# A two-layer encoder trunk in float32: gate projections by seven block products, up projections unit by unit, and memory products a step after their bank

## The chip, the cores and the metric

The kernel runs on one core of one Trainium2 chip. The metric is the device time in microseconds of one execution. Before the change the median of three runs is 2235.18 us (2234.59 to 2235.61).

## What is computed

Layer 0 is a mixer (a bidirectional mLSTM with 4 heads and a bidirectional RG-LRU) and a SwiGLU FFN, layer 1 is dilated sliding-window attention with 16 heads and a SwiGLU FFN. The change touches the FFN of both layers and the heads of the mLSTM. Cut to that:

```python
D_MODEL = 2048; SEQ = 256
D_FF = ((8 * D_MODEL + 3 * 256 - 1) // (3 * 256)) * 256      # 5632

def swiglu(h, w1, w3, w2):
    return (jax.nn.silu(h @ w1) * (h @ w3)) @ w2

def reference(x, ...):
    for l in range(DEPTH):                                   # DEPTH = 2
        ...                                                  # mixer or attention
        h = rmsnorm(x, f_norm[l])
        x = x + swiglu(h, f_w1[l], f_w3[l], f_w2[l])
    return rmsnorm(x, final_norm)

# in the mLSTM, for each head and direction
    s = jnp.einsum('bhld,bhsd->bhls', qj, kj) * w_intra
    num = jnp.einsum('bhls,bhsv->bhlv', s, vj) + ...
    h = num / jnp.maximum(jnp.abs(den), jnp.exp(-m_out))[..., None]
```

## The kernel before

All weights are float32. A weight block comes from memory as a unit `raw` of 512 rows by 512 columns (four row blocks of 128, 1 MB) and is split in two halves, each of two row blocks, into a high part `wh` (ACT casts it to fp32r, L205) and a low part `wl` (DVE subtracts, L206). Activations are held transposed and split in the same way, `xT`, with 256 tokens. A product is then three matmuls, high by high, high by low, low by high (`narrow`, L273 to L275): the stationary operand is a 128 by 128 block of the activations, the moving one 512 columns of the weights. One half of a unit is a **step**: two row blocks, two blocks of 128 tokens, three matmuls, twelve in all. Blocks whose output is wanted transposed go the other way round (L295, L296).

The program is written out step by step, and every engine runs its instructions in that order. `emit_step` (L277) first emits the splits up to three steps ahead (`AHEAD = 3`; `emit_split`, L192), then the step's matmuls, then it lets the open tasks run one piece each (`run_tasks`). The tasks are generators; a `yield` puts what follows behind the next step. What evacuates a chunk is such a task. The buffers of `wh` and `wl` are four each, so the split of step s + 4 waits for the matmuls of step s; those of `raw` are four too, and a load is issued on SP's queue when one is given back (`emit_load`).

An FFN (`ffn`, L920) has eleven chunks of 512 columns of w1 and w3. Chunk by chunk, all four units of w1 are taken, then all four of w3. `up1` (L924) evacuates w1: ACT applies Silu, scaled by the row norm `rstd`, into `up`. `up3` (L940) evacuates w3: DVE multiplies (L948), PE transposes (`hTp`), ACT and DVE split the result into `hT` (L961, L962). `UPS` cuts the eleven chunks into two passes, (0, 6) and (6, 11): after each, w2 is multiplied with the chunks made so far, for the four column groups of the output, and added to the residual `xres`. PSUM has eight banks: four for accumulators `acc` (two to a narrow chunk), two for transposes, two (`mx`) for small products, which a lock (`take`, `give`) hands from task to task.

In the mixer, `ml_head` (L673) makes for each head the products `qkp` and `nMb`, and later four products `num`. A task takes the lock, multiplies into the next of the two `mx` banks, reads the bank a step later and gives the lock back, then lets one step pass (`lag`).

Of the kernel before, what the change touches and what calls it, by code (L numbers as in the profile page):

```python
# [9 lines left out]
F32 = mybir.dt.float32  # L10
F32R = mybir.dt.float32r
AF = mybir.ActivationFunctionType
ALU = mybir.AluOpType
# [4 lines left out]
P = 128  # L18
KB = D // P
CW = 512  # L20
# [4 lines left out]
RB = 8  # L25
AH = 16
DH = 128
UPS = ((0, 6), (6, 11))
EPS = 1e-6
BIG = 1e30  # L30

# [3 lines left out]
C_N = 160  # L35


RAW_BUFS = 4
SPLIT_BUFS = 4
AHEAD = 3  # L40

SLOTS = 8
SLOT = 2112
EV_BUFS = 6
M4_BUFS = 6

CONC = 3
# [9 lines left out]
class Chunk:  # L57
    def __init__(self, evac):
        self.acc = None
        self.at_once = getattr(evac, "at_once", False)  # L60
        self.evac = evac

# [2 lines left out]
def trunk_kernel(ctx: ExitStack, tc: tile.TileContext, a, out):  # L65
# [37 lines left out]
    def mx(name="mx"):  # L103
        return mxp.tile([P, CW], F32, tag="mx", name=name)
# [3 lines left out]
    def lag():  # L108

        for _ in range(LAG):  # L110
            yield

    def take():

        while held["mx"]:
            yield
        held["mx"] = True
# [70 lines left out]
            pos["load"] += 1  # L188

    splits = {}  # L190

    def emit_split(s):  # L192

        st = steps[s]
        it = st["item"]
        raw = loaded[it][:, 2 * st["half"]:2 * st["half"] + 2, :]
        hi = whp.tile([P, 2, CW], F32R, tag="wh", name="wh")
        lo = wlp.tile([P, 2, CW], F32R, tag="wl", name="wl")
        for k in (0, 1) if s < 2 else (slice(0, 2),):
            if s < 2:  # L200
                use_xT(2 * s + k)
            elif s < KB // 2:
                use_xT(2 * s)
                use_xT(2 * s + 1)
            A.copy(hi[:, k], raw[:, k])  # L205
            V.tensor_tensor(lo[:, k], raw[:, k], hi[:, k].bitcast(F32), op=ALU.subtract)  # L206
        splits[s] = (hi, lo)
        if st["last_half"]:
            loaded.pop(it)
            emit_load()  # L210

    def add_unit(src, ch, kb0, first, last, act):

        items.append(wload(src, len(items)))
        it = len(items) - 1
        for h in range(2):
            steps.append({
                "item": it, "half": h, "last_half": h == 1, "ch": ch, "kb": kb0 + 2 * h, "act": act,
                "first": first and h == 0, "last": last and h == 1, "wide": False, "before": None,
            })  # L220

    def add_chunk(src, n_kg, act, evac, kgs=None):
        ch = Chunk(evac)
        for j, kg in enumerate(kgs or range(n_kg)):
            add_unit(src[kg], ch, 4 * kg, j == 0, j == n_kg - 1, act)
        return ch

    def add_blocks(units):

        for i in range(0, len(units), 2):  # L230
            pair = []
            for src, act, evac in units[i:i + 2]:
                items.append(wload(src, len(items)))
                pair.append((len(items) - 1, Chunk(evac), act))
            for h in range(2):
                for it, ch, act in pair:
                    steps.append({
                        "item": it, "half": h, "last_half": h == 1, "ch": ch, "kb": 8 * h, "act": act,
                        "first": h == 0, "last": h == 1, "wide": True, "before": None,
                    })  # L240

    urgent, queue, active = [], [], []
# [16 lines left out]
    def until(flag):  # L259
        n = 0  # L260
        while flag not in flags:
            run_tasks()
            n += 1
            assert n < 10000, flag

    def narrow(st, hi, lo, toks):
        for j in range(2):
            x2 = st["act"](st["kb"] + j)
            f, e = st["first"] and j == 0, st["last"] and j == 1
            for t in toks:  # L270
# [3 lines left out]
                PE.matmul(acc, xh, lo[:, j, :], start=False, stop=False)  # L274
                PE.matmul(acc, xl, hi[:, j, :], start=False, stop=e)  # L275

    def emit_step(s):  # L277
# [8 lines left out]
        hi, lo = splits.pop(s)  # L286
        if ch.acc is None:
            ch.acc = [accp.tile([P, CW], F32, tag="acc", name="acc") for _ in range(1 if st["wide"] else 2)]
        if st["wide"]:
            acc = ch.acc[0]  # L290
            wh, wl = (w.rearrange("p a (b f) -> p (a b) f", f=P) for w in (hi, lo))
            for j in range(8):
                x2 = st["act"](st["kb"] + j)
                f, e = st["first"] and j == 0, st["last"] and j == 7
                PE.matmul(acc, wh[:, j, :], x2.rearrange("p a b -> p (a b)"), start=f, stop=False)  # L295
                PE.matmul(acc[:, :S], wl[:, j, :], x2[:, 0, :], start=False, stop=e)  # L296
        else:
# [375 lines left out]
    def ml_head(h):  # L673
# [44 lines left out]
        for d in range(2):  # L718
            for t in range(2):
                yield from take()  # L720
                num = mx("num")[:, :DV + 1]
                pairs = [(3 * d + 2 * t, t)]
                if t != d:
                    pairs.append((3 * d + 1, d))
                for j, (blk, s) in enumerate(pairs):
                    PE.matmul(num, w6[:, blk, :], v[:, s, h, :DV + 1], start=j == 0, stop=j == len(pairs) - 1)  # L726
                yield
                r = sm(2, "den")
                V.tensor_scalar(
                    r[:, 0:1], num[:, DV:], -1.0, em[:, t, 4 * d + h:4 * d + h + 1], op0=ALU.mult, op1=ALU.max  # L730
                )
                V.tensor_tensor(r[:, 1:2], r[:, 0:1], num[:, DV:], op=ALU.max)
                V.reciprocal(r[:, 1:2], r[:, 1:2])
                hd = ml["h"][:, t, h, :]
                if d == 0:
                    A.mul(hd, num[:, :DV], r[:, 1:2])
                else:
                    V.scalar_tensor_tensor(hd, num[:, :DV], r[:, 1:2], hd, op0=ALU.mult, op1=ALU.add)
# [181 lines left out]
    def ffn(l, gains, nxt):  # L920
# [3 lines left out]
        def up1(c):  # L924
            def gen(ch):
                while f"rstd{gains}" not in flags:
                    yield
                es = []
                for t in range(2):
                    e = ev("up")  # L930
                    A.activation(e, ch.acc[t], AF.Silu, scale=cur["rstd"][:, t:t + 1])
                    es.append(e)
                ch.acc = None
                st["e", c] = es
                flags.add(f"up{l}_{c}")
                yield

            return gen
# [32 lines left out]
        def act_h(kb):  # L971
            until(f"h{l}_{kb}")
            return st["h", kb // 4][:, kb % 4]

        for hidx, (c0, c1) in enumerate(UPS):
# [3 lines left out]
            if hidx == 1:  # L979
                ssq = const.tile([P, 2, NCD], F32, name=f"ssq{l}")  # L980
            for n in range(NCD):
                if hidx == 0:
# [9 lines left out]
                add_chunk(a["w2"][l, n], c1 - c0, act_h, evac, kgs=range(c0, c1))  # L992
        return ssq


# [116 lines left out]
    n = NCD - 1  # L1112
    ch = steps[-1]["ch"]
    ends = [splits.pop(s) for s in range(len(steps) - tail, len(steps))]
    r = const.tile([P, 2], F32, name="rstd_f")
    for t in range(2):
        for st, (hi, lo) in zip(steps[-tail:], ends):
# [97 lines left out]
```

## Time and profile before

| | before |
|---|---|
| median of three runs | 2235.18 us |
| the profiled execution, its own time | 2238.2 us |
| its span | 2236.4 us |
| mean granted clock of TensorE | 0.996 |
| mixer up to the first FFN's first step | to about 375 us |
| FFN of layer 0, up to its last transposes | to about 1111 us |
| attention, up to the second FFN's first step | to about 1498 us |
| memory read over the span | 413.56 MB, 186 GB/s |

The stages are read from the transposes `nT`, which follow the last column group of each norm. PE is TensorE's matmul, PEld its weight load, DVE is VectorE, ACT ScalarE, POOL GpSimd, SP the engine that issues the loads. In a group of the profile stand the line, the engine, the operation, the tiles written and read, the shape and the count, then the busy time, the mean duration in ns, the idle time ahead of it and who ended that. In a timeline the first two numbers are start and duration in us. In a list of waits they are the total, the number and the longest in us. In a row of windows stand the window, its length, the busy time and number of instructions of each engine, the granted clock, the share of DMA and GB/s. In a row of loads stand the size of one load and the median time from issue to landing.

### The profile page before, as it was taken

The numbers are of one execution on the slowest core, as the hardware profiler recorded it, in microseconds if no ns is written. First come the engines' busy times: TensorE is split into PE (matmuls) and PEld (weight loads), VectorE is DVE, ScalarE is ACT, GpSimd is POOL, SyncE is SP. The second block draws the span as 40 slices with busy tenths as digits, with TensorE's granted clock in tenths as the row PEclk, the third lists the DMA queues.
The fourth block names the chain that finished last, engine by engine and source line by source line (L and its number), as shares of the span: only waits on it lengthen the run. The fifth ranks groups of instructions, "written<-read, shape, count | busy, mean of one in ns | idle before, by whom it ended". The sixth has DMA issues, their size and how long they took to land.

```text
span 2236.4 us, 25910 instructions
## 1 busy us (share of the span) xinstructions
PE 2217.9 (99%) x10412; PEld 1849.4 (83%) x10412; DVE 1246.7 (56%) x1516; ACT 1045.8 (47%) x1343; POOL 21.0 (1%) x37
## 2 busy tenths in 40 slices
PE   9999999999999999999999999999999999999998
PEld 7887888888888888888888888888888888888886
DVE  6876665445544444455566666564445444444554
ACT  6666545444443344444454555454444433444443
POOL 0000000000000000000000000000000000000000
PEclk9999999999999999999999999999999999999999
DMA  7443565555555555555555555555555556555553
GB/s 299 170 142 132 183 204 181 192 192 192 182 196 191 190 189 191 193 192 176 194 190 173 193 178 176 176 173 197 193 191 188 188 188 210 189 197 192 192 188 113
DMA packets 61457, 417.34 MB, mean 187 GB/s; under 512 B 7061, under 2 KB 7957, under 8 KB 12569
## 3 DMA queue, kind: packets, MB, share of 16 engines
q1 hardware_dynamic: 58616, 406.69, 53.4%
q0 software_dynamic: 2288, 8.39, 1.0%
q8 instruction: 81, 1.33, 0.2%
q10 hardware_dynamic: 432, 0.61, 0.1%
q14 instruction: 40, 0.32, 0.0%
HBM read 413.56 MB, written 2.10 MB: 186 GB/s over the span
## 4 chain that ended last, share of the span: by engine, by line
PE 94%; ACT 2%; DVE 2%; issue 1%; DMA 0%; SPq 0%; POOL 0%; POOLq 0%; DVEq 0%; ACTq 0%
PE acc L273 26%; PE acc L275 26%; PE acc L274 26%; PE acc L295 9%; PE acc L296 4%; ACT wh L205 1%; PE hTp L142 1%; DVE wl L206 1%; PE rgp L456 0%; PE nT L142 0%; PE apT L142 0%; DMA raw<-in_w_v 0%; PE num L726 0%; DVE xres L346 0%; PE asc L862 0%
## 5 line engine op out<-in xcount | busy, mean ns | idle before, releaser
L206 DVE TENSOR_TENSOR wl<-raw,wh 128x1024 fp32r<-128x1024 f32 (+1 forms) x770 | 940.4, 1222 | 851.6 <-ACT wh L205 849.2
L205 ACT CAST wh<-raw 128x1024 fp32r<-128x1024 f32 (+1 forms) x770 | 806.1, 1049 | 876.5 <-PE acc L275 795.0
L273 PE MATMUL acc<-wh,xT 128*128 128x512 f32 x1664 | 658.1, 396 | 0.9 <-ACT wh L205 0.9
L274 PE MATMUL acc<-wl,xT 128*128 128x512 f32 x1664 | 650.8, 391 | 1.2 <-DVE wl L206 1.2
L275 PE MATMUL acc<-wh,xT 128*128 128x512 f32 x1664 | 650.9, 391 | 0.0
L273 PEld LDWEIGHTS acc<-wh,xT 128*128 128x128 f32 x1664 | 313.8, 189 | 66.5 <-ACT wh L205 1.6
L274 PEld LDWEIGHTS acc<-wl,xT 128*128 128x128 f32 x1664 | 314.0, 189 | 65.9 <-DVE wl L206 2.6
L275 PEld LDWEIGHTS acc<-wh,xT 128*128 128x128 f32 x1664 | 313.6, 188 | 66.1
L295 PE MATMUL acc<-xT,wh 128*128 128x512 f32 x896 | 322.1, 402 | 0.5 <-ACT v L663 0.5
L273 PE MATMUL acc<-wh,hT 128*128 128x512 f32 x704 | 275.5, 391 | 0.0
L275 PE MATMUL acc<-wh,hT 128*128 128x512 f32 x704 | 274.4, 390 | 0.0
L274 PE MATMUL acc<-wl,hT 128*128 128x512 f32 x704 | 274.2, 389 | 0.0
L296 PE MATMUL acc<-xT,wl 128*128 128x256 f32 x896 | 251.7, 281 | 0.0
L295 PEld LDWEIGHTS acc<-xT,wh 128*128 128x128 f32 x896 | 168.5, 188 | 40.0 <-ACT v L663 0.6
L296 PEld LDWEIGHTS acc<-xT,wl 128*128 128x128 f32 x896 | 169.6, 189 | 0.9 <-DVE wl L206 0.3
L275 PEld LDWEIGHTS acc<-wh,hT 128*128 128x128 f32 x704 | 132.2, 188 | 27.5
L274 PEld LDWEIGHTS acc<-wl,hT 128*128 128x128 f32 x704 | 132.2, 188 | 27.2
L273 PEld LDWEIGHTS acc<-wh,hT 128*128 128x128 f32 x704 | 132.2, 188 | 27.0
L961 ACT CAST hT<-hTp 128x512 fp32r<-128x512 f32 x44 | 25.8, 587 | 83.2 <-PE hTp L142 83.2
L962 DVE TENSOR_TENSOR hT<-hTp,hT 128x512 fp32r<-128x512 f32 x44 | 30.4, 692 | 55.1 <-ACT hT L961 55.1
L273 PE MATMUL acc<-wh,oT 128*128 128x512 f32 x128 | 50.7, 396 | 0.0
L275 PE MATMUL acc<-wh,oT 128*128 128x512 f32 x128 | 50.0, 391 | 0.0
(222 smaller groups left out, 1206.4 us busy)
## 6 DMA issues: line engine op xcount, KB each, us to landing
raw<-in_w SPq DMA_DIRECT2D x264, 1024.0 KB, 4.8
raw<-in_w_aqk SPq DMA_DIRECT2D x32, 1024.0 KB, 4.8
raw<-in_w_out SPq DMA_DIRECT2D x16, 1024.0 KB, 4.9
raw<-in_w_av SPq DMA_DIRECT2D x16, 1024.0 KB, 4.8
raw<-in_w_o SPq DMA_DIRECT2D x16, 1024.0 KB, 4.8
raw<-in_w_xr SPq DMA_DIRECT2D x8, 1024.0 KB, 6.4
raw<-in_w_qk SPq DMA_DIRECT2D x8, 1024.0 KB, 4.8
raw<-in_w_og SPq DMA_DIRECT2D x8, 1024.0 KB, 4.9
```

What stands on the lines that cost most here:

```text
L142: PE.transpose(o, i, ident[:n, :n])
L205: A.copy(hi[:, k], raw[:, k])
L206: V.tensor_tensor(lo[:, k], raw[:, k], hi[:, k].bitcast(F32), op=ALU.subtract)
L273: PE.matmul(acc, xh, hi[:, j, :], start=f, stop=False)
L274: PE.matmul(acc, xh, lo[:, j, :], start=False, stop=False)
L275: PE.matmul(acc, xl, hi[:, j, :], start=False, stop=e)
L295: PE.matmul(acc, wh[:, j, :], x2.rearrange("p a b -> p (a b)"), start=f, stop=False)
L296: PE.matmul(acc[:, :S], wl[:, j, :], x2[:, 0, :], start=False, stop=e)
L961: A.copy(h[:, 2 * p:2 * p + 2, 0, :], ps)
L962: V.tensor_tensor(h[:, 2 * p:2 * p + 2, 1, :], ps, h[:, 2 * p:2 * p + 2, 0, :].bitcast(F32), op=ALU.subtract)
```

## The change

**Gate projections.** For the chunks 1 to 10 of w1 and the last three of its four units (`SEVEN`), a step is a 2 by 2 block product (two blocks of tokens, two row blocks, two halves of 256 columns) by Winograd's form of Strassen's scheme: seven block products in place of eight, each three matmuls of 256 columns. Four sums of weight blocks are made per unit (`weight_sums`; one stays in `raw`, three are split into `wf`), and four sums of activation blocks once per layer (`act_sums`, split into `sf`). Two further accumulators `ext` hold the shared products, and `up1` joins the four before Silu.

**Order of the up projections.** Units of w1 and w3 alternate; the accumulators of w3 lie in the two `mx` banks. `UPS` has four passes. In each, the last chunk's units of w2 come after the others' for the first two column groups.

**Buffers.** `raw` three for four, `ev` ten for six. The final gain is loaded 16 steps before the end and not 90.

**Memory products.** In `ml_head` the `lag` stands behind `take` and no longer behind `give`, and there is one more ahead of `qkp`.

```diff
-UPS = ((0, 6), (6, 11))
+UPS = ((0, 3), (3, 6), (6, 9), (9, 11))
+SEVEN = (1, 2, 3)
-RAW_BUFS = 4
+RAW_BUFS = 3
-EV_BUFS = 6
+EV_BUFS = 10
...
+    def weight_sums(it):
+        w = loaded[it]
+        b11, b12, b21, b22 = (w[:, i::2, 256 * j:256 * j + 256] for i in range(2) for j in range(2))
+        t1, t2, t4 = ts = [ev("ws").rearrange("p (a b) -> p a b", a=2) for _ in range(3)]
+        V.tensor_tensor(t1, b12, b11, op=ALU.subtract)
+        V.tensor_tensor(b12, b22, b12, op=ALU.subtract)
+        V.tensor_tensor(t2, b22, t1, op=ALU.subtract)
+        V.tensor_tensor(t4, b21, t2, op=ALU.subtract)
+        sums[it] = []
+        for t in ts:
+            f = m4((4, 256), "wf", F32R).rearrange("p (i a) b -> p i a b", i=2)
+            A.copy(f[:, 0], t)
+            V.tensor_tensor(f[:, 1], t, f[:, 0].bitcast(F32), op=ALU.subtract)
+            sums[it].append(f)
...
     def emit_split(s):
+        if st["seven"] and st["half"] == 0:
+            weight_sums(it)
...
+        todo = [
+            (a(a1, 0), b(0, 0), e0, 0), (sa(0), tb(0), e0, 1), (sa(1), tb(1), e1, 0), (sa(2), b(0, 1), e1, 1),
+            (a(a2, 0), b(1, 0), c0, 0), (sa(3), b(1, 1), c0, 1), (a(a2, 1), tb(2), c1, 0),
+        ]
+        for (xh, xl), (wh, wl), dst, n in ([todo[k] for k in (1, 0, 3, 2, 5, 4, 6)] if st["last"] else todo):
+            o = dst[:, n * 256:n * 256 + 256]
...
+            PE.matmul(o, xh, wh, start=new, stop=False)
+            PE.matmul(o, xh, wl, start=False, stop=False)
+            PE.matmul(o, xl, wh, start=False, stop=end)
...
         yield from take()
+        yield from lag()
         ps = mx("qkp")
...
                 yield from take()
+                yield from lag()
                 num = mx("num")[:, :DV + 1]
...
                 give()
-                yield from lag()
...
+                if ch.ext:
+                    A.copy(x0, e0)
+                    V.tensor_tensor(u2, e1[:, l_], x0[:, l_], op=ALU.add)
+                    V.tensor_tensor(x1[:, l_], e1[:, r_], u2, op=ALU.add)
+                    V.tensor_tensor(x1[:, r_], x1[:, l_], x0[:, r_], op=ALU.add)
+                    V.tensor_tensor(x0[:, r_], x0[:, r_], u2, op=ALU.add)
+                    V.tensor_tensor(x0, c0, x0, op=ALU.add)
+                    V.tensor_tensor(x1, c1, x1, op=ALU.add)
...
+        def act_sums():
+            for g in SEVEN:
...
+                for j, kb in enumerate((4 * g, 4 * g + 2)):
+                    V.tensor_tensor(vv, x[:, :, 0, :], x[:, :, 1, :], op=ALU.add)
+                    V.tensor_tensor(w[:, 0], a21, a22, op=ALU.add)
+                    V.tensor_tensor(w[:, 2], a11, a21, op=ALU.subtract)
+                    V.tensor_tensor(w[:, 1], w[:, 0], a11, op=ALU.subtract)
+                    V.tensor_tensor(w[:, 3], a12, w[:, 1], op=ALU.subtract)
+                    A.copy(f[:, :, 0, :], w)
+                    V.tensor_tensor(f[:, :, 1, :], w, f[:, :, 0, :].bitcast(F32), op=ALU.subtract)
+                    yield
...
-                add_chunk(a["w1"][l, c], 4, act, up1(c))
-                add_chunk(a["w3"][l, c], 4, act, up3(c))
+                for g in range(4):
+                    add_unit(a["w1"][l, c][g], chs[0], 4 * g, g == 0, g == 3, act,
+                             seven if c and g in SEVEN else None)
+                    add_unit(a["w3"][l, c][g], chs[1], 4 * g, g == 0, g == 3, act)
...
+            for n, kgs in ((0, range(c0, c1 - 1)), (1, range(c0, c1 - 1)), (0, (c1 - 1,)), (1, (c1 - 1,)),
+                           (2, range(c0, c1)), (3, range(c0, c1))):
...
+        steps[at_first]["before"] = lambda: queue.append(act_sums())
...
-    steps[-90]["before"] = load_fg
+    steps[-16]["before"] = load_fg
```

The emitted order shows the change at three places. The first is DVE at the start of the first FFN. The rows `xT` are the last norm's transposes being split, and each `wl` is the split of one step. Before:

```order
L346 TENSOR_TENSOR xres<-acc,xres 128x512 x2
L206 TENSOR_TENSOR wl<-raw,wh 128x1024
L373 SCALAR_TENSOR_TENSOR xT<-nT,cpk,xT 128x256 x4
L380 TENSOR_REDUCE rstd_3182<-ssq_o_115 128x2
L381 TENSOR_SCALAR rstd_3182<-rstd_3182 128x2
L206 TENSOR_TENSOR wl<-raw,wh 128x1024 x16
```

And now (`sa`, `sb` and `sf` belong to the sums of the activations):

```order
L441 SCALAR_TENSOR_TENSOR xT<-nT,cpk,xT 128x256 x4
L448 TENSOR_REDUCE rstd_3180<-ssq_o_115 128x2
L449 TENSOR_SCALAR rstd_3180<-rstd_3180 128x2
L1067 TENSOR_TENSOR sa<-xT 128x512
L1070 TENSOR_TENSOR sb<-sa 128x128
L1071 TENSOR_TENSOR sb<-sa 128x128
L1072 TENSOR_TENSOR sb<-sb,sa 128x128
L1073 TENSOR_TENSOR sb<-sa,sb 128x128
L1075 TENSOR_TENSOR sf<-sb,sf 128x4x128
L229 TENSOR_TENSOR wl<-raw,wh 128x1024
```

The rows from `sa` to `wl` follow six times; one set of sums now stands ahead of each of the splits of the FFN's steps 4 to 9, where sixteen splits followed each other before.

The second is DVE behind the end of a chunk (`up` is the gating, `hT` the split of the transposed result). Before:

```order
L206 TENSOR_TENSOR wl<-raw,wh 128x1024 x16
L948 SCALAR_TENSOR_TENSOR up<-acc,rstd_3182,up 128x512 x2
L206 TENSOR_TENSOR wl<-raw,wh 128x1024 x2
L962 TENSOR_TENSOR hT<-hTp,hT 128x2x256
L206 TENSOR_TENSOR wl<-raw,wh 128x1024
```

And now, from the joining of the accumulators on (`ws` and `wf` are the sums of weight blocks and their split):

```order
L1008 TENSOR_TENSOR up<-acc,up 128x512
L1009 TENSOR_TENSOR up<-acc,up 128x512
L229 TENSOR_TENSOR wl<-raw,wh 128x1024 x2
L1027 SCALAR_TENSOR_TENSOR up<-acc,rstd_3180,up 128x512 x2
L202 TENSOR_TENSOR ws<-raw 128x512
L203 TENSOR_TENSOR raw<-raw 128x2x256
L204 TENSOR_TENSOR ws<-raw,ws 128x512
L205 TENSOR_TENSOR ws<-raw,ws 128x512
L210 TENSOR_TENSOR wf<-ws,wf 128x512 x3
L229 TENSOR_TENSOR wl<-raw,wh 128x1024 x2
L1041 TENSOR_TENSOR hT<-hTp,hT 128x2x256
```

Six additions (the last two are shown) come ahead of two splits, and seven instructions between the gating and the next split.

The third is PE in the mixer, between the last `num` of one head and the `qkp` and `nMb` of another, where `nMb` goes into the bank that this `num` was in. Before, the rows that end the step between them:

```order
L273 MATMUL acc_1622<-wh_1550,xT_99 128x512
L274 MATMUL acc_1622<-wl_1551,xT_99 128x512
L275 MATMUL acc_1622<-wh_1550,xT_99 128x512
L682 MATMUL qkp_1664<-qkT_981 128x256 x2
L685 MATMUL nMb_1667<-nMs_798,ehr_97 128x512 x2
```

And now:

```order
L300 MATMUL acc_1604<-wh_1671,xT_99 128x512
L301 MATMUL acc_1604<-wl_1672,xT_99 128x512
L302 MATMUL acc_1604<-wh_1671,xT_99 128x512
L524 MATMUL rgp_1778<-xc_469,rgw_1442 128x256 x2
L751 MATMUL qkp_1784<-qkT_979 128x256 x2
L754 MATMUL nMb_1787<-nMs_796,ehr_97 128x512 x2
```

Before, `num_1640` stands twelve matmuls of `acc` ahead of `qkp_1664`. Now `num_1721` stands 24 ahead of `qkp_1784`, with two pairs of `rgp` (the RG-LRU's gates) between.

More of the change, by code (lines that the diff above doesn't have):

```diff
@@ L59, in __init__ @@
         self.acc = None
+        self.ext = None
+        self.small = False
         self.at_once = getattr(evac, "at_once", False)
@@ L207, in emit_split @@
         splits[s] = (hi, lo)
+        if st["seven"]:
+            splits[s] = (hi, lo, [t[:, :, st["half"]] for t in sums[it]])
+            if st["last_half"]:
+                sums.pop(it)
         if st["last_half"]:
@@ L210, in emit_split, with add_unit @@
             emit_load()
-    def add_unit(src, ch, kb0, first, last, act):
+    def add_unit(src, ch, kb0, first, last, act, seven=None):
         items.append(wload(src, len(items)))
@@ L218, in add_unit @@
                 "item": it, "half": h, "last_half": h == 1, "ch": ch, "kb": kb0 + 2 * h, "act": act,
-                "first": first and h == 0, "last": last and h == 1, "wide": False, "before": None,
+                "first": first and h == 0, "last": last and h == 1, "wide": False, "before": None, "seven": seven,
             })
@@ L238, in add_blocks @@
                         "item": it, "half": h, "last_half": h == 1, "ch": ch, "kb": 8 * h, "act": act,
-                        "first": h == 0, "last": h == 1, "wide": True, "before": None,
+                        "first": h == 0, "last": h == 1, "wide": True, "before": None, "seven": None,
                     })
@@ L275, in narrow, with seven_products, a, sa @@
                 PE.matmul(acc, xl, hi[:, j, :], start=False, stop=e)
+    def seven_products(st, hi, lo, ts):
+        ch = st["ch"]
+        a1, a2 = (st["act"](st["kb"] + j) for j in range(2))
+        sf = st["seven"](st["kb"])
+        if ch.ext is None:
+            ch.ext = [accp.tile([P, CW], F32, tag="acc", name="ext") for _ in range(2)]
+            ch.opened = set()
+        (c0, c1), (e0, e1) = ch.acc, ch.ext
+        def a(x, t):
+            return x[:, 0, t * P:(t + 1) * P], x[:, 1, t * P:(t + 1) * P]
+        def sa(k):
+            return sf[:, k, 0, :], sf[:, k, 1, :]
+        def b(j, n):
+            return hi[:, j, n * 256:n * 256 + 256], lo[:, j, n * 256:n * 256 + 256]
+        def tb(k):
+            return ts[k][:, 0, :], ts[k][:, 1, :]
+        todo = [
[4 more added lines that the diff above has]
+            o = dst[:, n * 256:n * 256 + 256]
+            new = dst is not c0 and dst is not c1 and id(dst) not in ch.opened
+            ch.opened.add(id(dst))
+            end = st["last"] and n == 0
+            PE.matmul(o, xh, wh, start=new, stop=False)
+            PE.matmul(o, xh, wl, start=False, stop=False)
+            PE.matmul(o, xl, wh, start=False, stop=end)
     def emit_step(s):
@@ L285, in emit_step @@
         ch = st["ch"]
-        hi, lo = splits.pop(s)
+        hi, lo, *ts = splits.pop(s)
         if ch.acc is None:
-            ch.acc = [accp.tile([P, CW], F32, tag="acc", name="acc") for _ in range(1 if st["wide"] else 2)]
+            if ch.small:
+                ch.acc = [mx("acc") for _ in range(2)]
+            else:
+                ch.acc = [accp.tile([P, CW], F32, tag="acc", name="acc") for _ in range(1 if st["wide"] else 2)]
         if st["wide"]:
@@ L296, in emit_step @@
                 PE.matmul(acc[:, :S], wl[:, j, :], x2[:, 0, :], start=False, stop=e)
+        elif st["seven"]:
+            seven_products(st, hi, lo, *ts)
         else:
@@ L927, in gen @@
                     yield
-                es = []
+                es = [ev("up") for t in range(2)]
+                if ch.ext:
+                    (c0, c1), (e0, e1) = ch.acc, ch.ext
+                    l_, r_ = slice(0, 256), slice(256, CW)
+                    x0, x1 = es
+                    u2 = ev("u2")[:, l_]
+                    A.copy(x0, e0)
[5 more added lines that the diff above has]
+                    V.tensor_tensor(x1, c1, x1, op=ALU.add)
                 for t in range(2):
[L930 to L933, printed above, removed]
+                    A.activation(es[t], es[t] if ch.ext else ch.acc[t], AF.Silu, scale=cur["rstd"][:, t:t + 1])
+                ch.acc = ch.ext = None
                 st["e", c] = es
@@ L1114, in trunk_kernel @@
     ends = [splits.pop(s) for s in range(len(steps) - tail, len(steps))]
+    if ch.acc is None:
+        ch.acc = [accp.tile([P, CW], F32, tag="acc", name="acc") for _ in range(2)]
     r = const.tile([P, 2], F32, name="rstd_f")
```

29 lines of the change are left out of this document (26 added, 3 removed).

## The prediction

> **What bounds the kernel now.** The page comes first, its shares of busy time and its chain of work that ended last, then its two costliest groups off TensorE:
>
> ```profile
> PE 2217.9 (99%) x10412; PEld 1849.4 (83%) x10412; DVE 1246.7 (56%) x1516; ACT 1045.8 (47%) x1343; POOL 21.0 (1%) x37
> ...
> PE 94%; ACT 2%; DVE 2%; issue 1%; DMA 0%; SPq 0%; POOL 0%; POOLq 0%; DVEq 0%; ACTq 0%
> ...
> L206 DVE TENSOR_TENSOR wl<-raw,wh 128x1024 fp32r<-128x1024 f32 (+1 forms) x770 | 940.4, 1222 | 851.6 <-ACT wh L205 849.2
> L205 ACT CAST wh<-raw 128x1024 fp32r<-128x1024 f32 (+1 forms) x770 | 806.1, 1049 | 876.5 <-PE acc L275 795.0
> ```
>
> TensorE is 94% of the chain. The two engines that split the weights wait for it (795.0 us of ACT's idle time before the split ends with a matmul), so matmul time removed is time won, as long as DVE and ACT keep up. A busy PE can still be stalled behind a modelled end, so I read the pace from starts, in the timeline of PE: first twelve 512-column products of the second FFN projection, then six 256-column products of an attention score, which also load a new stationary block each.
>
> ```profile
> 1000.20 0.39 PE L275 MATMUL acc<-wh,hT 128*128 128x512 f32 x1
> ...
> 1002.92 0.39 PE L275 MATMUL acc<-wh,hT 128*128 128x512 f32 x1
> ```
> ```profile
> 1150.54 0.28 PE L860 MATMUL asc<-aqk 128*128 128x256 f32 x1
> ...
> 1151.26 0.40 PE L295 MATMUL acc<-xT,wh 128*128 128x512 f32 x1
> ```
>
> (1002.92 - 1000.20)/12 = 0.2267 us for 512 columns; (1151.26 - 1150.54)/6 = 0.120 us for 256. The extra fixed time per product is therefore about 0.013 us, and halving the columns nearly halves the time.
>
> **1. The seven products: -24.0 us.** A step of the gate projection is 12 x 0.2267 = 2.720 us now and 21 x 0.120 = 2.520 us then: 0.200 less. Such steps are the chunks 1 to 10, three of four units, two halves, two layers: 10 x 3 x 2 x 2 = 120; the built order has 1080 = 120 x 9 more matmuls. 120 x 0.200 = 24.0. Rounding of the two starts (0.01 in 0.72) makes this 20 to 28.
>
> The Trainium skill, "TensorE: Matmul & The Clock Gate", section "Back-to-back issue gap", gives N/2.4 + 2.5 ns, 109 and 216 ns; an estimate by it is 0.29 us a step and 35 us. The starts above are 11 ns longer for both widths, and the measured ones decide.
>
> **2. Does DVE keep up in a chunk?** The chain's list gives the period of a chunk of w1 with its w3 (16 steps and 8 transposes); groups and timeline give the pieces:
>
> ```profile
> 427.89 0.44 PE hTp L142 x4
> ...
> 472.38 0.44 PE hTp L142 x4
> ```
> ```profile
> L948 DVE SCALAR_TENSOR_TENSOR up<-acc,rstd,up 128x512 f32<-128x512 f32 x44 | 30.9, 744 | 0.0
> L962 DVE TENSOR_TENSOR hT<-hTp,hT 128x512 fp32r<-128x512 f32 x44 | 30.4, 692 | 55.1 <-ACT hT L961 55.1
> L931 ACT ACTIVATE up<-acc,rstd 128x512 f32<-128x512 f32 x44 | 27.7, 681 | 0.0
> ...
> L961 ACT CAST hT<-hTp 128x512 fp32r<-128x512 f32 x44 | 25.8, 587 | 83.2 <-PE hTp L142 83.2
> ...
> L349 ACT ACTIVATE sqj<-xres 128x512 f32<-128x512 f32 x30 | 18.7, 625 | 26.9 <-DVE xres L346 26.9
> ...
> L833 DVE SCALAR_TENSOR_TENSOR aqk<-aqk,rb 128x256 f32<-128x256 f32 x32 | 13.6, 425 | 1.1
> ...
> L354 DVE TENSOR_TENSOR xres<-xres,fg 128x512 f32<-128x512 f32 x6 | 3.9, 686 | 0.0
> ```
>
> The period is 44.49 now and 44.49 - 6 x 0.200 = 43.29 then. DVE in it: 16 splits x 1.22 = 19.5; three weight sums of seven 512-wide instructions x 0.69 = 14.5; joining the four accumulators, four of 256 (0.43) and two of 512 (0.69) = 3.1; and as before 2 x 0.744 + 2 x 0.692 = 2.9. Sum 40.0, 92%. ACT has 16 x 1.05 + 9 copies x 0.63 + 3 x 0.59 + 2 x 0.68 = 25.6. Two more numbers make 40.0 an upper value: DVE runs two independent instructions in less than their sum,
>
> ```profile
> 374.83 1.28 DVE L346 TENSOR_TENSOR xres<-acc,xres 128x512 f32<-128x512 f32 x2
> ...
> 382.37 2.36 DVE L206 TENSOR_TENSOR wl<-raw,wh 128x1024 fp32r<-128x1024 f32 x2 [0.18 <-ACT wh L205]
> ```
>
> so some 0.08 is saved at a hand-over. A split is made three steps ahead, and the tightest is the first one behind weight sums after a chunk's end. Take 0 at the end of w1's last step. ACT and DVE first split for a later step (done at 2.3); DVE then joins the accumulators, 3.0 less overlaps: the first is free at 4.6, the second at 5.2. The next chunk writes them at 5.44 and 6.1, after two steps of w3. ACT's two Silus end at 6.0, its two casts at 7.9; DVE's two splits at 9.4, the gating of w3 at 10.7, the weight sums 4.4 later, the split that they delay at 16.3. Its step starts at 6 x 2.72 + 8 x 0.11 = 17.2. The lead is 0.9 us there and more later in the chunk, as no joining comes before it. So I cost the weight sums and the joining at **0**: matmuls cover them. If 0.1 us were lost at each of some 40 hand-overs instead, DVE would need 44.0 a chunk, 0.7 to 0.8 us above 43.29, and 20 such chunks lose 16 us.
>
> **3. The sums of the activations: +18.2 us.** They are made once per layer, six times in a row, in the first steps of the FFN. There DVE has just worked off the last norm. Timeline of DVE, then ACT, then the group of a 128-wide instruction:
>
> ```profile
> 377.86 1.22 DVE L206 TENSOR_TENSOR wl<-raw,wh 128x1024 fp32r<-128x1024 f32 x1 [1.75 <-ACT wh L205]
> 379.00 0.48 DVE L373 SCALAR_TENSOR_TENSOR xT<-nT,cpk,xT 128x256 fp32r<-128x256 f32 x1
> ...
> 382.02 0.17 DVE L381 TENSOR_SCALAR rstd<-rstd 128x2 f32<-128x2 f32 x1
> ```
> ```profile
> 376.79 1.03 ACT L205 CAST wh<-raw 128x1024 fp32r<-128x1024 f32 x1
> ```
> ```profile
> L326 DVE TENSOR_SCALAR dg<-cst,rstd 128x128 f32<-128x128 f32 x2 | 0.5, 282 | 0.0
> ```
> ```profile
> 377.85 1.03 PE L142 MATMUL nT<-cst,xres 128*128 128x128 f32 x8
> 378.64 0.47 PE L273 MATMUL acc<-wh,xT 128*128 128x512 f32 x1
> ```
>
> The split for the FFN's step 3 ends at 379.1; the first activation sum can start at 382.15. In the new order each one stands ahead of one split on both engines. One turn: the 512-wide add 0.72, four 128-wide ones, of which three hang on one another, 1.05; ACT's cast 0.62, behind it ACT's cast of the weights 1.05 (DVE's own difference, 0.69, lies beside it); then the split 1.22; hand-overs +0.04 (376.79 + 1.03 to 377.86) twice and -0.15 where neighbours overlap. 4.6 us, where PE takes 2.72. The split of step 4 is ready at 382.15 + 4.6 = 386.8, just in time (378.6 + 3 x 2.72 = 386.8); the three-step lead is used up. Each of the next five comes 1.87 us later against PE than the one before, less 0.3 since a step's first product does without the low part: 5 x 1.87 - 0.3 = 9.1 us in each layer. Two layers: 18.2. From below this is 0 (if ACT overtook the chain), from above 28, see the first rival; I take 18.2, being worked from this place's own rows.
>
> **4. Memory products a step later: -10.2 us.** The list of PE's waits and windows of PE:
>
> ```profile
> PE num L726 <- ACT hacc L736: 3.4, 1, 3.4
> PE nMb L685 <- DVE hacc L738: 2.2, 1, 2.2
> ```
> ```profile
> 180.00:185.00 5.00, 5.00 (x13) 0.50 0.64 210
> 185.00:190.00 5.00, 5.00 (x23) 0.99 0.00 0
> 227.40:232.40 5.00, 5.00 (x13) 0.50 0.52 165
> ```
> ```profile
> 183.77 0.63 PE L274 MATMUL acc<-wl,xT 128*128 128x512 f32 x1
> ...
> 184.62 0.60 PE L273 MATMUL acc<-wh,xT 128*128 128x512 f32 x1
> ```
>
> After each of the two waits the granted clock is 0.50 for 5 us: products start 0.425 apart, 13 where 23 fit, and 10 x 0.2267 = 2.3 us are lost again. 3.4 + 2.2 + 2 x 2.3 = 10.2. Now 12 matmuls lie between a product and the reuse of its bank at the first place, 24 then and two small products; 24 x 0.2267 = 5.4 covers the 2.7 + 2.2 = 4.9 that the reading took. At the second place the distance in one bank grows from 36 to 48 matmuls, 2.7 us of the 3.4, and the scan work that held DVE there no longer falls between the same products. The last memory output moves by seven steps and still lies ten steps ahead of its reader. Bounds: 0 (both waits move to another product) to 12 (with the edges of the two slow stretches).
>
> **5. The rest: 0.** Four passes over w2 in place of two add adds of 0.68 us on DVE in steps that carry one split of 1.22 per 2.72. Three raw buffers in place of four: a 1 MB load lands in 4.8 us,
>
> ```profile
> raw<-in_w SPq DMA_DIRECT2D x264, 1024.0 KB, 4.8
> fg<-in_final_norm POOLq DMA_DIRECT2D x1, 1024.0 KB, 5.2
> ```
>
> and by the times of part 2 a buffer is freed at least 8 us before its next split, 3 us more than the load takes; without that cover each load costs up to 4.8. At the start the constants (0.3 MB) pass item 3 in SP's queue, 1.6 us at this rate, against a lead of up to three steps. The final gain is issued 16 steps before the end; its first use comes six steps later, 16 us, and the load needs 5.2.
>
> **The sum.** The profiled execution took 2238.2 (span 2236.4 and 1.8 around it). 2238.2 - 24.0 - 10.2 + 18.2 = 2222.2. The median of the runs, 2235.2, is 3.0 below that execution: **2219.2**, 0.7% faster. Its own range is 2211 to 2227, from the first and third terms.
>
> **Rivals.**
> - *The clock halves at the start of each FFN.* For: 0.50 after waits of 2.2 and 3.4 us. Against: here each gap is 1.9 us in a turn of 4.6. At half clock a step takes 12 x 0.425 = 5.1; 0.5 more in five steps and 2.3 for the return, 4.9 a layer: 2219 + 10 = 2229. The Trainium skill, "TensorE: Matmul & The Clock Gate", section "Why this matters for your kernels", warns of idle gaps over about 3 us; by it these gaps are harmless. The trace disagrees, it halves already after 2.2 us, so 1.9 is near the point: chance 0.15.
> - *The activation sums are hidden.* If the turn is near 3 us, 2219 - 18 = 2201. For: DVE's own work in it is 3.9 us, and PE leads by only little. Against: the turn hangs on ACT. 0.15.
> - *The mixer's waits only move*: 2219 + 10 = 2229. For: the same bank pair, a longer hold. Against: the distances above. 0.07.
> - *DVE is the bound in the chunks*: 2219 + 16 = 2235. For: 92%. Against: the overlaps. 0.09.
> - *Slower: loads are no longer hidden behind 256 columns.* A weight load is recorded with 189 ns,
>
> ```profile
> L861 PEld LDWEIGHTS asc<-aqk 128*128 128x128 f32 x32 | 6.0, 189 | 0.2
> ```
>
> more than the 120 ns between products; runs of six are all that this trace has, and a run of 21 or 42 might fall back on the load. The point is 2.720/21 = 0.1295 us a product. At 0.14 a step costs 2.94: 120 x 0.42 = 50 us more, 2269; at 0.189 it is far worse. Against: the six starts are evenly spaced, so two loads overlap. 0.09.
>
> **Numbers.** Forecast 0.45. A change of 0.2% (4.5 us) is about what a measurement of this kernel can tell from none: faster ends at 2230.7. The two rivals at 2229 straddle it and give 0.13 to faster and 0.09 to same. Faster 0.45 + 0.15 + 0.13 = 0.73; same 0.09 + 0.06 of the DVE rival = 0.15; slower 0.12. 2199 to 2238 leaves out the slower tail and an edge of the hidden case.
>
> **What would show it.** Starts 0.12 apart within the seven products; about 43.3 between the transposes of neighbouring chunks; PE waiting on wl some 9 us in the first ten steps of each FFN, with the clock at 1.00; no wait at num and nMb above 0.5, and no window of 0.50 there. The forecast is wrong if products stand more than 0.125 apart, if PE waits on wl or wf inside later chunks, or if the FFN's start keeps its 2.72 a step.

## The result, and the profile after

| | before | after |
|---|---|---|
| median of four runs, us | 2235.39 (2234.59 to 2236.57) | 2223.69 (2223.18 to 2224.18) |
| ratio after/before | | 0.9947, 95% interval 0.9932 to 0.9962 |
| the profiled execution, its own time and span, us | 2238.2, 2236.4 | 2224.16, 2222.4 |
| mean granted clock | 0.996 | 0.999 |

The change is 0.5% faster; 2219.2 was forecast. Of all the runs in this document one is left out, an execution in the first experiment with more work in the activation sums, which took 2414.59 us at a granted clock of 0.85. The page of after, with its busy times, its chain of work by engine and its two costliest groups off TensorE:

```profile
PE 2195.4 (99%) x11492; PEld 1875.3 (84%) x11492; DVE 1592.0 (72%) x2160; ACT 1156.2 (52%) x1555; POOL 22.6 (1%) x37
...
PE 91%; DVE 4%; ACT 3%; issue 1%; DMA 0%; SPq 0%; POOL 0%; POOLq 0%; DVEq 0%; ACTq 0%
...
L229 DVE TENSOR_TENSOR wl<-raw,wh 128x1024 fp32r<-128x1024 f32 (+1 forms) x770 | 927.7, 1220 | 512.1 <-ACT wh L228 508.1
L228 ACT CAST wh<-raw 128x1024 fp32r<-128x1024 f32 (+1 forms) x770 | 793.9, 1046 | 500.5 <-PE acc L302 364.8
```

PE has 1080 matmuls more and is busy 22.5 us less; DVE has 345 us more work, 72% where it had 56%. PE's share of the chain fell from 94% to 91%, and DVE's and ACT's rose: there is a new place where PE waits for them.

To see where the time went, I set the transposes that follow the last column group of a norm against each other; they close the mixer, the first FFN and the attention. Timeline of PE (start, duration), first after, then before (its first mark, 377.85, stands in the prediction):

```profile
367.85 0.81 PE L146 MATMUL nT<-cst,xres 128*128 128x128 f32 x6
...
1098.32 0.33 PE L146 MATMUL nT<-cst,xres 128*128 128x128 f32 x1 [0.20 <-DVE xres L414]
...
1489.30 0.92 PE L146 MATMUL nT<-cst,xres 128*128 128x128 f32 x7
```
```profile
1110.38 0.82 PE L142 MATMUL nT<-cst,xres 128*128 128x128 f32 x6
...
1500.73 0.82 PE L142 MATMUL nT<-cst,xres 128*128 128x128 f32 x6
```

| stage, us | before | after | difference | forecast |
|---|---|---|---|---|
| mixer | 377.9 | 367.9 | -10.0 | -10.2 |
| first FFN | 732.5 | 730.5 | -2.1 | -12.0 + 9.1 |
| attention | 390.4 | 391.0 | +0.6 | 0 |
| second FFN, to the end of the span | 735.7 | 733.1 | -2.6 | -12.0 + 9.1 |

From one profiled execution to the other the change gains 14.0; the sum of the prediction was 16.0.

**The seven products.** Timeline of PE in the first FFN: a product of one step and the same product of the next, 21 starts later. Then the window between two chunks' transposes:

```profile
430.24 0.28 PE L337 MATMUL ext<-wl,xT 128*128 128x256 f32 x1
...
432.75 0.28 PE L337 MATMUL ext<-wl,xT 128*128 128x256 f32 x1
```
```profile
426.65:469.94 43.29, 43.29 (x257) 38.41 (x255) 36.01 (x45) 22.79 (x29) 0.00 (x0) 1.00 0.56 194
```

(432.75 - 430.24)/21 = 0.1195 us; counted over all 2460 neighbouring starts in such steps it is 0.1202. The period is 43.29 us, which was forecast to the last digit. The 189-ns weight loads stay hidden in runs of 42 products too. DVE is busy 36.0 us (83%) where 40.0 was reckoned: 45 of a chunk's 47 instructions lie in this window, and they overlap their neighbours by 2.2 us together, which the prediction mentions (0.08 at a hand-over) and didn't subtract.

**The start of the FFN.** PE, then ACT, then DVE over one turn of the activation sums, and windows of PE (us, busy, granted clock):

```profile
384.56 0.49 PE L300 MATMUL acc<-wh,xT 128*128 128x512 f32 x1 [0.47 <-ACT wh L228]
...
385.82 0.50 PE L301 MATMUL acc<-wl,xT 128*128 128x512 f32 x1 [0.77 <-DVE wl L229]
...
389.07 0.49 PE L300 MATMUL acc<-wh,xT 128*128 128x512 f32 x1 [0.47 <-ACT wh L228]
```
```profile
382.93 0.62 ACT L1074 CAST sf<-sb 128x512 fp32r<-128x512 f32 x1 [2.95 <-DVE sb L1073]
383.46 1.04 ACT L228 CAST wh<-raw 128x1024 fp32r<-128x1024 f32 x1
```
```profile
381.16 0.68 DVE L1067 TENSOR_TENSOR sa<-xT 128x512 f32<-128x512 f32 x1
...
383.59 0.69 DVE L1075 TENSOR_TENSOR sf<-sb,sf 128x512 fp32r<-128x512 f32 x1 [0.69 <-ACT sf L1074]
384.54 1.23 DVE L229 TENSOR_TENSOR wl<-raw,wh 128x1024 fp32r<-128x1024 f32 x1 [0.26 <-ACT wh L228]
385.68 0.68 DVE L1067 TENSOR_TENSOR sa<-xT 128x512 f32<-128x512 f32 x1
```
```profile
380.00:400.00 20.00, 14.26 (x52) 1.00 0.31 106
400.00:420.00 20.00, 20.00 (x90) 1.00 0.73 262
```

The turn is 389.07 - 384.56 = 4.51 us, where PE needs 2.72, and it can be read off as a chain: the sums on DVE end at 382.9, ACT casts them (0.62), then casts the weights (1.04), DVE makes the low part (1.23), and only then starts the next sums. Five such turns in each layer cost 5 x 1.79 = 8.95 us; the clock stays at 1.00. PE is held up twice in a turn, ahead of the high part (0.47 us idle) and ahead of the low part (0.77). From the norm's last transposes to the first transposes of a chunk it is 58.64 us (367.85 to 426.49), where before it was 49.88 (377.85 to 427.73): 8.76 longer, and the same in the second layer.

**The mixer.** List of PE's waits of after (total, number, longest), and two windows, the first of PE alone, the second of all engines:

```profile
PE acc L301 <- DVE wl L229: 9.1, 14, 0.8
PE acc L300 <- ACT wh L228: 4.8, 12, 0.5
PE num L796 <- ACT q L763: 1.4, 1, 1.4
PE nT L146 <- DVE xres L414: 1.1, 5, 0.3
```
```profile
183.00:188.00 5.00, 5.00 (x24) 1.00 0.35 146
```
```profile
214.00:224.00 10.00, 8.62 (x42) 6.97 (x41) 9.06 (x16) 5.64 (x9) 0.00 (x0) 1.00 0.40 138
```

The first two rows belong to the starts of the FFNs, all but some 2 us; they count only idle time, less than the turns lose. Both waits of before (3.4 and 2.2) are gone, and so are the stretches at 0.50. A smaller wait of 1.4 us has come in at a `num`, in a stretch where DVE is 91% busy; the clock holds through it.

### The profile page after: what moved, and what is told of

It reads as the page before. It is cut to its first block, busy times and chain, and to the rows that moved or that the text cites. A ratio compares the mean times of both kernels' runs of the same rounds, so it can differ in the third digit from the quotient of the medians.

```text
span 2222.4 us, 28893 instructions
## 1 busy us (share of the span) xinstructions
PE 2195.4 (99%) x11492; PEld 1875.3 (84%) x11492; DVE 1592.0 (72%) x2160; ACT 1156.2 (52%) x1555; POOL 22.6 (1%) x37
## 4 chain that ended last, share of the span: by engine, by line
PE 91%; DVE 4%; ACT 3%; issue 1%; DMA 0%; SPq 0%; POOL 0%; POOLq 0%; DVEq 0%; ACTq 0%
PE acc L301 20%; PE acc L302 20%; PE acc L300 20%; PE acc L361 9%; PE acc L362 5%; PE ext L337 3%; PE ext L338 3%; PE ext L336 3%; PE acc L337 2%; PE acc L336 2%; PE acc L338 2%; DVE wl L229 2%; ACT wh L228 2%; PE hTp L146 1%; PE rgp L524 1%
## 5 line engine op out<-in xcount | busy, mean ns | idle before, releaser
L229 DVE TENSOR_TENSOR wl<-raw,wh 128x1024 fp32r<-128x1024 f32 (+1 forms) x770 | 927.7, 1220 | 512.1 <-ACT wh L228 508.1
L228 ACT CAST wh<-raw 128x1024 fp32r<-128x1024 f32 (+1 forms) x770 | 793.9, 1046 | 500.5 <-PE acc L302 364.8
L300 PE MATMUL acc<-wh,xT 128*128 128x512 f32 x1184 | 468.0, 395 | 4.9 <-ACT wh L228 4.8
L301 PE MATMUL acc<-wl,xT 128*128 128x512 f32 x1184 | 463.5, 391 | 9.1 <-DVE wl L229 9.1
L302 PE MATMUL acc<-wh,xT 128*128 128x512 f32 x1184 | 461.3, 390 | 0.0
L301 PEld LDWEIGHTS acc<-wl,xT 128*128 128x128 f32 x1184 | 222.6, 188 | 56.0 <-DVE wl L229 13.9
L300 PEld LDWEIGHTS acc<-wh,xT 128*128 128x128 f32 x1184 | 222.6, 188 | 55.1 <-ACT wh L228 10.4
L302 PEld LDWEIGHTS acc<-wh,xT 128*128 128x128 f32 x1184 | 222.3, 188 | 46.7
L209 ACT CAST wf<-ws 128x512 fp32r<-128x512 f32 x180 | 111.9, 622 | 197.6 <-DVE ws L202 149.0
L210 DVE TENSOR_TENSOR wf<-ws,wf 128x512 fp32r<-128x512 f32 x180 | 113.3, 684 | 0.0
L338 PE MATMUL ext<-wf,sf 128*128 128x256 f32 x240 | 67.9, 283 | 0.0
L337 PE MATMUL ext<-wf,sf 128*128 128x256 f32 x240 | 67.9, 283 | 0.0
```

Source lines behind the costliest of these rows:

```text
L209: A.copy(f[:, 0], t)
L210: V.tensor_tensor(f[:, 1], t, f[:, 0].bitcast(F32), op=ALU.subtract)
L300: PE.matmul(acc, xh, hi[:, j, :], start=f, stop=False)
L337: PE.matmul(o, xh, wl, start=False, stop=False)
L338: PE.matmul(o, xl, wh, start=False, stop=end)
```

## The experiments

All are edits of the changed kernel. Where an edit adds instructions, nobody reads their results.

**A yield in the activation sums.** The sums on DVE and the cast on ACT are put on either side of a step.

```diff
                     V.tensor_tensor(w[:, 3], a12, w[:, 1], op=ALU.subtract)
+                    yield
                     A.copy(f[:, :, 0, :], w)
```

> The changed kernel with one more yield in the sums of the activations: the additions of one set are emitted in one step, ACT's cast and DVE's difference of it in the next. Theory (PE waits at the start of each FFN because six sets, each a chain DVE, ACT, ACT, DVE of 4.6 us, stand ahead of six splits in six steps): with two steps of 5.44 us for a set and ACT no longer waiting for the additions, the waits go, 8.9 us in each layer; 2223.7 - 17.9 = 2206, and PE's waits on wl and wh fall from 14 to about 4 us. Rival (the waits come from the norm's last transposes, or from three raw buffers): the time stays within 2 us of 2223.7.

Measured: 2205.63 us (2205.12 to 2206.22, four runs), ratio to before 0.9869 (0.9855 to 0.9882). That is 18.1 us under the changed kernel, as against 2 x 8.95 = 17.9 read from its turns. PE's waits on `wh` and `wl` fall from 13.9 us to 1.6. Timeline of DVE, and windows of all engines from the FFN's start:

```profile
372.96 0.29 DVE L1073 TENSOR_TENSOR sb<-sa,sb 128x128 f32<-128x128 f32 x1
373.17 1.22 DVE L229 TENSOR_TENSOR wl<-raw,wh 128x1024 fp32r<-128x1024 f32 x1
374.30 0.69 DVE L1076 TENSOR_TENSOR sf<-sb,sf 128x512 fp32r<-128x512 f32 x1
374.91 1.22 DVE L229 TENSOR_TENSOR wl<-raw,wh 128x1024 fp32r<-128x1024 f32 x1
376.04 0.69 DVE L1067 TENSOR_TENSOR sa<-xT 128x512 f32<-128x512 f32 x1
```
```profile
366.00:386.00 20.00, 20.00 (x94) 16.64 (x93) 17.37 (x33) 11.64 (x17) 1.08 (x1) 1.00 0.47 159
386.00:406.00 20.00, 20.00 (x90) 16.56 (x89) 15.21 (x25) 10.33 (x11) 0.00 (x0) 1.00 0.62 210
```

DVE now runs a split between the sums and their own split, and waits for ACT at neither, so six sets of sums pass while PE never stops. The work is the same; the whole loss was in the order of a chain that went from DVE to ACT's two casts and back to DVE.

**The memory products' lag put back.**

```diff
         yield from take()
-        yield from lag()
         ps = mx("qkp")
...
                 yield from take()
-                yield from lag()
                 num = mx("num")[:, :DV + 1]
...
                 give()
+                yield from lag()
```

> The changed kernel with the mixer's lag where it was before. Theory (the change of order there is worth the two waits at nMb and num and the half clock behind them, 10 us): the two waits are back, a window at 0.50 behind each, and the time is 2223.7 + 10 = 2234. Rival (the mixer's end comes earlier through three raw buffers or the alternating FFN, not through the lag): within 2 us of 2223.7.

Measured: 2231.57 (2229.11 to 2232.76, eleven runs), ratio 0.9982 (0.9973 to 0.9991); 7.9 us above the changed kernel. Its list of waits, then windows of PE from edge to edge of its slow stretches, first here and then in the profile of before:

```profile
PE num L794 <- ACT hacc L804: 3.4, 1, 3.4
PE nMb L753 <- DVE hacc L806: 1.9, 1, 1.9
```
```profile
179.40:182.81 3.41, 3.41 (x10) 0.50 0.74 245
182.81:223.77 40.96, 38.72 (x171) 1.00 0.31 108
223.77:230.60 6.83, 5.51 (x13) 0.50 0.34 110
```
```profile
178.24:185.07 6.83, 6.83 (x16) 0.50 0.47 155
185.07:226.03 40.96, 38.06 (x168) 1.00 0.30 103
226.03:232.86 6.83, 6.17 (x15) 0.50 0.45 152
```

Both waits and a lower clock behind each are back, so the lag is what removed them. The first stretch is half as long as in the profile of before, though, 3.41 us and not 6.83; the second is as long. How long the clock stays down thus differs between executions that wait alike. Kernels with these two waits scatter by 3.7 us (this one) and 4.8 (before, 2232.97 to 2237.75 in 19 runs), those in which the clock stays up by about 1.

**No seven products.** Eight block products throughout; the order of the units, the passes, the buffers and the lag stay.

```diff
-SEVEN = (1, 2, 3)
+SEVEN = ()
```

> The changed kernel with no unit by seven products and no sums, everything else kept (alternating units, w3 in the small banks, four passes, three raw buffers, the lag). Theory (seven products save 24.0, their sums cost 17.9 at the two starts and nothing in the chunks): 2223.7 + 24.0 - 17.9 = 2230. If the alternating order or the four passes cost or gave something by themselves, the difference shows: without any, the time before less the mixer's 10 us would be 2225. So 2230 says that the rest of the change costs some 5 us, 2225 that the seven products net nothing.

Measured: 2229.32 (2228.89 to 2230.05, nine runs), ratio 0.9974 (0.9964 to 0.9983). The seven products with their sums are worth 5.6 us as they stand (24.0 - 17.9 = 6.1 by the traces). And all the rest of the change gives 2235.3 - 2229.3 = 6.0, of which the lag is 7.9: what the prediction put at nothing costs some 2 us.

**More work in the weight sums,** one or three idle subtractions of 512 columns in each:

```diff
         V.tensor_tensor(t4, b21, t2, op=ALU.subtract)
+        d = ev("dm").rearrange("p (a b) -> p a b", a=2)
+        for _ in range(3):                  # or range(1)
+            V.tensor_tensor(d, b21, b11, op=ALU.subtract)
```

One:

> The changed kernel with one idle 512-wide subtraction (0.7 us) added to every weight sum, where three were tried before. Theory (the lead of 1.1 and 1.4 us is what covers DVE): 0.7 is inside the first lead, 2 x 0.7 just at the second one; at most 0.2 us in a chunk, 2224 to 2228. Rival (each extra microsecond on DVE costs its full time, as 54 us for three would suggest by a straight line): 18 us, 2242.

Three:

> The changed kernel with three idle 512-wide subtractions on DVE added to every weight sum (60 units; some 2 us each, nothing reads their result). Theory (DVE is not the bound, but the first split behind weight sums after a chunk's end has a lead of only 1.1 us and the second 1.4): PE now waits some 0.7 to 0.9 us at the first and 1.5 at the second in most chunks, 35 to 45 us in all, 2260 to 2270. Rival (DVE, 72% busy, has a wide margin): under 2230. Rival (DVE is the bound already): 60 x 2 = 120 us more, 2340.

Measured: with one 2223.54 (2223.41 to 2223.82), ratio 0.9945 (0.9932 to 0.9959), no cost. With three 2277.99 (2277.68 to 2278.47), ratio 1.0193 (1.0179 to 1.0207), 54.3 us above the changed kernel and more than was expected. The lead behind this, in the changed kernel: DVE's weight sums and the splits behind them, and the matmul that reads the first of these splits:

```profile
466.75 0.68 DVE L202 TENSOR_TENSOR ws<-raw 128x512 f32<-128x512 f32 x1
...
471.20 2.36 DVE L229 TENSOR_TENSOR wl<-raw,wh 128x1024 fp32r<-128x1024 f32 x2
```
```profile
473.53 0.28 PE L337 MATMUL ext<-wl,xT 128*128 128x256 f32 x1
```

The first of the two splits takes 1.23 and ends at 472.43, 1.10 us ahead of its reader. None of the 60 leads is under 1.09; behind the second weight sums of the same chunk it is 1.39, behind the third 2.45. One subtraction (0.69) fits, three (2.07) don't. With one the lead behind the second weight sums, which both additions delay, falls from 1.39 to 0.20, so little room is left for two. A window of one chunk with one more, one from a chunk's transposes to the next with three more, and the wait of the latter:

```profile
426.70:469.99 43.29, 43.29 (x256) 38.40 (x255) 37.70 (x49) 22.77 (x29) 0.00 (x0) 1.00 0.56 195
```
```profile
470.53:517.25 46.72, 44.09 (x255) 38.45 (x254) 42.47 (x54) 24.66 (x30) 0.00 (x0) 1.00 0.51 181
```
```profile
PE ext L340 <- DVE wl L232: 39.9, 58, 1.5
```

With three this period is 46.72 where it was 43.29, and from mark to mark each FFN is 27.6 us longer (758.1 and 760.6, where the changed kernel took 730.5 and 733.1). I had taken each delayed split by itself, two of three late; 58 of the 60 are late, since DVE, whose 42.47 would fill 98% of the old period, no longer catches up between one set of sums and the next.

**More work in the activation sums,** to lengthen PE's gap and see what the clock does. First on DVE:

```diff
+                    d = ev("dm")
+                    for _ in range(2):
+                        V.tensor_tensor(d, v, v, op=ALU.add)
                     A.copy(f[:, :, 0, :], w)
```

> The changed kernel with two idle 512-wide additions (1.3 us together) on DVE in each sum of the activations, so that PE's idle time in each turn at the start of an FFN grows from 1.7 to about 3 us. If the clock stays at 1.00: six turns of 1.3 us in each layer, 2223.7 + 16 = 2240. If it halves, as behind the waits of 2.2 and 3.4 us in the mixer: a window at the start of the FFN shows a granted clock well under 1, and since the turn still hangs on DVE and ACT, only the return costs, up to 2.3 us a layer more: 2240 to 2245.

Measured: 2225.76 in the middle of three runs (2225.58 to 2226.65), ratio 0.9956 (0.9941 to 0.9971). The expectation was wrong: 1.3 us more work a turn made it only 0.2 us longer. ACT's cast doesn't wait for these additions, so they lie beside its two casts (1.66 us, in which DVE had only 0.69 to do), and DVE is now busy through the whole turn. In the changed kernel the turn hangs on ACT's chain. So the next edit put the work there:

```diff
+                    d = ev("dm")
+                    for _ in range(2):
+                        A.copy(d, w.rearrange("p k t -> p (k t)"))
                     A.copy(f[:, :, 0, :], w)
```

> The changed kernel with two idle 512-wide copies on ACT (some 1.1 us together) ahead of ACT's cast in each sum of the activations. The last run showed that two idle additions on DVE at this place are mostly hidden (a turn grew by 0.2 us), so the turn should hang on ACT's casts. Theory: these copies lie in that chain, a turn grows from 4.5 to 5.6 us, and 6 x 1.1 us in each of two layers come on top, 2223.7 + 13 = 2237; PE is then idle some 2.8 us in a turn. If idle time as such sets the granted clock, as behind the waits of 2.2 and 3.4 us in the mixer, the window from 380 to 400 shows a clock well under 1; if it stays at 1.00, the length of a gap alone does not decide. Rival (the turn hangs on DVE): under 2228.

Measured: 2238.52 (2236.89 to 2240.39, ten runs), ratio 1.0011 (1.0002 to 1.0021), 14.8 us above the changed kernel. PE at the start of two turns of the first FFN, then windows of PE from edge to edge of the slow stretches, two in the first FFN and two in the second:

```profile
392.35 0.50 PE L300 MATMUL acc<-wh,xT 128*128 128x512 f32 x1 [1.62 <-ACT wh L228]
...
398.04 0.50 PE L300 MATMUL acc<-wh,xT 128*128 128x512 f32 x1
```
```profile
383.44:386.85 3.41, 3.06 (x8) 0.50 0.71 288
386.85:393.68 6.83, 3.77 (x14) 1.00 0.01 2
393.68:397.09 3.41, 3.41 (x8) 0.50 0.70 235
1516.66:1520.07 3.41, 3.41 (x9) 0.50 0.00 0
1533.73:1537.14 3.41, 3.41 (x9) 0.50 0.78 252
```

The turn is 398.04 - 392.35 = 5.69 us, 1.17 more, so it does hang on ACT. From the norm's last transposes to the first of a chunk the first FFN takes 65.68 us where the changed kernel took 58.64: 7.0 more, which is six times 1.17 and not five, as the first set of sums is no longer hidden either. With 3.0 of 5.7 us lost in a turn the clock does come down, which it didn't with 1.8 of 4.5, but only in some turns. In the first FFN that costs nothing: the turn shown holds a slow stretch and is no longer than one without, as PE has time to spare in it. In the second FFN the last stretch lies behind the last of these waits, and this start takes 67.27 us, 1.6 more than the first, about half of that stretch. The runs scatter by 3.5 us.

**Other passes.** The last pass before w2 gets three chunks and the third two.

```diff
-UPS = ((0, 3), (3, 6), (6, 9), (9, 11))
+UPS = ((0, 3), (3, 6), (6, 8), (8, 11))
```

> The changed kernel with the passes (0,3), (3,6), (6,8), (8,11): the last pass has three chunks, so that the last norms of a layer lie two steps further apart for each column group. Theory (the two microseconds that the forecast lacks are lost there, since the last pass of two chunks crowds the norms' evacuations): PE's waits at the transposes nT fall and the time is 1 to 2 us under 2223.7. Rival (they are lost elsewhere): within 0.5 us of 2223.7.

Measured: 2222.93 (2222.84 to 2223.19, five runs), ratio 0.9942 (0.9929 to 0.9956), 0.8 us under the changed kernel. PE's waits between 1040 and 1120 us, at the last norm of layer 0, in the changed kernel and in this one (before had none there):

```profile
PE nT L146 <- DVE xres L414: 0.7, 3, 0.3
```
```profile
PE nT L146 <- DVE xres L414: 0.2, 1, 0.2
```

So a part of the 2 us is the last additions to `xres` coming late for the norm: the attention takes 390.5 us here where it took 391.0, and the first FFN 730.3 for 730.5. But the second FFN is 0.7 longer (733.8 for 733.1), and the rest of this execution's lead lies in the mixer, which the edit leaves alone. The passes move the loss more than they remove it, and the 0.8 of the medians isn't explained by the stages.

**The yield and these passes together.**

> The additional yield in the sums of the activations and the passes (0,3), (3,6), (6,8), (8,11) together: 2205.6 less what the passes alone bring, 2204 to 2206.

Measured: 2205.34 (2205.26 to 2205.98, four runs), ratio 0.9864 (0.9851 to 0.9878). This and the yield alone, 0.3 us apart, beat both kernels: 1.4% under before, 0.8% under the change.

## Why the prediction was right, and where it was off

**Seven products, -24.0.** As forecast: 0.1202 us a product, a chunk of 43.29, and 12.0 in each layer. The clearest support is the period, which holds nothing but this term; without the seven products it is 44.49 again. The rival in which the weight loads come to light at 256 columns is refuted by the 2460 starts. The estimate by the Trainium skill, "TensorE: Matmul & The Clock Gate", section "Back-to-back issue gap", would have made it 36 (the prediction's 0.29 us a step is 0.30 when it is worked out); the traces keep the 11 ns more per product that the attention's products had shown.

**DVE keeps up, 0.** Right in its result. The tightest lead was put at 0.9 and is 1.10. The reckoned 40.0 us a chunk left out overlaps of 2.2, and DVE's share is not the whole answer: 37.7 of 43.29 costs nothing, three more instructions a weight sum cost 54 us. The rival with DVE as the bound is not what happens here, but it lies only two or three instructions a weight sum away.

**Activation sums, +18.2.** Right: five turns a layer, 4.51 where 4.6 was forecast, 8.95 us each layer where 9.1 was, the clock at 1.00. The sign named for it showed only in part: the list has 9.1 us of waits on `wl` for both layers together and 4.8 on `wh`, where some 9 on `wl` in each layer were expected. PE is held up twice in a turn and not once. The undoing experiment gives 18.1. That the turn hangs on ACT, which was given as the reason against the rival "hidden", was tested from both sides: of 1.3 us more on DVE beside ACT's casts the turn took up 0.2, of two copies on ACT (some 0.62 each) 1.17. The rival "the clock halves" took the loss of a turn as one gap of 1.9 us; it is two shorter ones. It did not happen at 1.8 us lost in a turn, and did in some turns at 3.0; there it cost 1.6 us in one place and nothing in the others that the trace shows.

**Memory products, -10.2.** The mechanism is right: the lag alone removes both waits and the lower clock behind them. In the profiled executions the mixer gained 10.0, but it is luck that this comes so near. The slow stretches of before last 6.83 us each, not 5, and PE is busy in 13.0 us of them, so half of that, 6.5, was lost there and not 4.6. Against it stands a new wait of 1.4 that the prediction had excluded ("no wait at num and nMb above 0.5"). And the end of this mixer lies between 366.4 and 367.9 in the profiles of the nine kernels that have it. In medians the lag is worth 7.9.

**The last step of the sum, -3.0.** This is the step that failed, and 2.5 of the 4.5 us by which the forecast was off. The prediction carried the distance between the profiled execution of before and its median over to the new kernel. But that distance was no constant. Of the 19 runs of before beside the first experiments, two with a mean granted clock of 0.999 took 2232.97 and 2233.84, nine at 0.998 2233.46 to 2235.66, seven at 0.997 2235.17 to 2236.64, and one at 0.996 2237.75: the profiled execution, 0.996 and 2238.2, is one in which the clock stayed down long after the two waits (6.83 us twice, as against 3.41 and 6.83 in the profile with the lag put back). The change takes these waits away, all runs of after have 0.999, and its profiled execution lies only 0.5 above its median. Without this step the sum is 2222.2 for an execution that took 2224.16.

**The rest, 0.** It cost 2: +0.6 in the attention, +1.0 and +0.5 in the FFNs beside the two terms above, and 1.9 by the two experiments on the lag and the products. With it the sum comes to 2224.2. The kernel without the seven products has the same +0.5 in the attention and +1.0 and +0.6 in the FFNs, so this belongs to the order of the units, the passes or the buffers. The other passes took 0.5 from the attention and gave 0.7 to the second FFN; what the three raw buffers or the order of the units cost was not tried and stays open.

## What to carry to other kernels

Where helper work is put ahead of a steady stream of splits, look at the chain of one turn across engines, not at each engine's sum: here one yield, so that an engine has other work between handing over and taking back, was worth more than three times the net gain of the arithmetic that it served. And when a profiled execution lies above the median of its runs, find out why before that distance is carried to another kernel: if it comes from a wait that the change removes, it goes with it.

## What the runs showed of the hardware that was not expected

The granted clock does not follow the length of one gap alone. A wait of 1.9 to 2.2 us and one of 3.4 each went with a stretch at 0.50; a single wait of 1.4 did not, nor did the turns of 4.5 us in which PE lost 1.8 in two shorter gaps, or those of 4.7 with 2.0 lost (two more additions on DVE). Where 3.0 of 5.7 us were lost in two gaps, it came down in some turns and not in others. All these slow stretches are 3.41 or 6.83 us long, and which it is differs between executions of one order of work: after the same wait the profile of before has 6.83 and the one with the lag put back 3.41. Kernels with the two waits scatter by 3.7 to 4.8 us and their times follow their mean clocks; those in which the clock stays up scatter by about 1 us. What decides whether the clock comes down is not shown.
